# A hybrid attention layer on one core: first piece of x in two halves, a shorter warm-up, own raw buffers for the MLP weights, and other numbers in the order planner

## The chip, the cores and the metric

The kernel runs on one core of one Trainium2 chip. The metric is the time of one execution on the device in microseconds (us), of which three were taken. The profile is of one more execution, whose own time stands beside its span (the time from the first to the last instruction of the program).

## The reference: what is computed

One layer of a decoder over 512 tokens of width 1024, in float32. The input x is scaled by an RMS norm and projected once; the 3420 columns of the projection are split between two groups of eight heads of 64 that work side by side.

Group A is a native sparse attention. Each query attends three times: to 31 compressed keys, to selected blocks of 64 keys, and to a sliding window. With 512 tokens there are 8 blocks and up to 16 may be selected, and the window is 512 long, so that both of the last two are plain causal attention with keys and values of their own. The compressed keys and values come from two small networks (MLPs): 32 tokens of 64 numbers are put in a row, multiplied by a 2048 x 256 matrix, passed through SiLU and multiplied by a 256 x 64 matrix. Sigmoid gates weigh the three results.

Group B attends to the 128 keys per query that an indexer picks: four small heads of q x k, a relu, a weighted sum of the heads, then the 128 largest.

```
proj = rms_norm(x, norm_gain) @ w_in
o_nsa = g0 * o_cmp + g1 * o_sel + g2 * o_win;   o_nsa = o_nsa * silu(z_n)
score = sum_h relu(qi_h @ ki.T * 64**-0.5) * wi_h * 4**-0.5;   keys = top_k(score, 128)
o_dsa = attention(qd, kd[keys], vd[keys]) * silu(z_d)
out = x + concat(o_nsa, o_dsa) @ w_out
```

Queries and keys have an RMS norm and rotary positions.

## The kernel before, in words

Every product is made of three: each operand is split into a high part, rounded to the fp32r type by a copy, and a low part, the difference. High times high, high times low and low times high are added in PSUM. So each weight that arrives in a raw buffer costs one ScalarE copy (the high part, L356) and one subtraction on GpSimd or VectorE (the low part, L357) before TensorE can use it.

The program starts with the projection I (the indexer's keys and queries, L479). x arrives already transposed, in eight blocks k of 128 rows, each in one row with the 348 columns of the weights I for that block. The first block comes as one transfer with the norm's gains (`xw0`, L454), the others in five transfers (L352). For each block ScalarE makes the high part of x times gain (L466), ScalarE the square of x (L469), VectorE the running sum of the squares (L471), VectorE the low part (L473), and both the two parts of the weights (L475, L476); then come twelve products, for four tiles of 128 tokens. Ten products on a tile of zeros (`WARM`, L443) run on TensorE before the first block is there. The sum of the squares gives the norm's scale, which is applied to results later on.

After that the program projects chunks of columns in turn: C (input of the MLPs), B (keys and values of group A), Q1 and Q2 (queries), D, and Z0 to Z3 (the gates of the output). Between them stand the MLPs (`hidden`, L776, with the weights that `load_w1` brings in eight pieces of 256 KB for each of the two networks), the indexer (L689 to L704), attention, and at the end the output projection (L1219) with its own weights. Raw weights share one ring of four buffers (`raw`, `RAWB`); the MLPs' split weights have four tiles of four blocks each for both networks together, so that the second network's can be written only as the first's have been used.

Attention goes through units (a kind, a tile of 128 queries, a group of heads). For each unit the scores (L1010) are masked, exponentiated (L987) and scaled (L1000), the probabilities are transposed on TensorE (L1029), copied to a high part `pth` by ScalarE (L1030, or L1025 for the compressed keys) and a low part `ptl` (L1031), and multiplied with the values (L1040). `pth` and `ptl` have `TBUFS` buffers each. Mixed tiles (`mx`, L1198 to L1200) go into the output projection.

The order of the instructions is not that of the text. `set_order` (L112 onwards) collects all instructions with their dependences, those through the rings of buffers too, and plays the program forwards and backwards several times with a cost for each instruction, a latency between each pair of engines and a model of the transfers; each engine takes the ready instruction that is due first. The numbers above the function weigh this: `SPARE` is extra time between a producer and a product on TensorE, `PORT` a charge for VectorE and GpSimd when they want the port that they share, `SOON` how far ahead an engine looks for something more pressing, `PAUSE` a gap in the interleaving of the indexer. The best order found is made fixed: within each engine the instructions run in exactly that order, and a late operand holds up all that stands behind it. SyncE (SP) issues all the transfers, in one queue and in such an order too.

Of the kernel before, what the change touches and what calls it, by code (L numbers as in the profile page):

```python
# [9 lines left out]
F32 = mybir.dt.float32  # L10
# [3 lines left out]
AF = mybir.ActivationFunctionType  # L14
# [48 lines left out]
ARENA = 3689  # L63
ARENA_R = 5376 - 1024

WARM = 10
RTB = 4

COST = 1 / 2400
TBUFS, AHEAD, LAG = 3, 2, 2  # L70
R0, X0, L0 = 1.0, 0.5, 2.0
RA, X1, X2, X3, X4 = 0.2, 0.32, 0.4, 0.5, 0.2
PAUSE, LEAD, RAWB, W1B = 2.0, 8.0, 4, 8

MAGIC = float(0x5F3759DF)

# [7 lines left out]
    ("SP", "PE"): 900, ("SP", "DVE"): 950, ("SP", "Activation"): 900, ("SP", "Pool"): 950,  # L84
}

URGENT, SOON = 3000, 300
PE_URGENT, PE_SOON = 200, 60
ROUNDS = 8

# [2 lines left out]
LO_DVE = {"C": range(2)}  # L93

WBUFS = 4
PORT = 10

TURN = {"Activation": 125, "DVE": 118}

CHOICE = 0.0  # L100

SPARE = 200

HURRY = {}

# [3 lines left out]
def set_order(tc):  # L109
# [120 lines left out]
    def turns(due, back=False):  # L230


        to, frm = (before, after) if back else (after, before)
        left = [len(b) for b in frm]
        ready = [0.0] * count
        idle = defaultdict(float)
        waiting = defaultdict(list)
        for k in range(count):
            if not left[k]:
                waiting[eng[k]].append(k)  # L240
        order = defaultdict(list)
        start = [0.0] * count
        last = {e: () for e in TURN}
        if not back:
            due = [d - h for d, h in zip(due, hurry)]
            for k in reversed(range(count)):
                for j in before[k]:
                    due[j] = min(due[j], due[k] - costs[j][0])
        there = [0.0] * LANES
        for _ in range(count):  # L250
            now, e = min((max(idle[e], min(ready[k] for k in l)), e) for e, l in waiting.items() if l)
            l = waiting[e]

            late = max(idle["port"] - now, 0)
            k = min((k for k in l if ready[k] <= now), key=lambda k: due[k] + PORT * late * port[k]
                    + (CHOICE * TURN[e] if e in TURN and rows[k] != last[e] else 0))
            soon, urgent = (PE_SOON, PE_URGENT) if e == "PE" else (min(SOON, costs[k][0]), URGENT)

            u = min((q for q in l if now < ready[q] < now + soon), key=lambda q: due[q], default=None)
            if u is not None and due[u] + urgent < due[k]:  # L260
                k = min((q for q in l if ready[q] <= now and now + costs[q][0] <= ready[u] + 50),
                        key=lambda q: due[q], default=u)
            l.remove(k)
            start[k] = max(idle[e], ready[k], idle["port"] if port[k] else 0)
            if by[k] == "SP" and not back:
                start[k] = max(start[k], there[0])
            more = 0
            if e in TURN:
                if rows[k] != last[e]:
                    more = max(TURN[e] - (start[k] - idle[e]), 0)  # L270
                last[e] = rows[k]
            end = idle[e] = start[k] + costs[k][0] + more
            if port[k]:
                idle["port"] = end
            if by[k] == "SP":
                if back:
                    idle["transfers"] = max(idle["transfers"], start[k]) + costs[k][1]
                    end = max(end, idle["transfers"]) + 650
                else:
                    end = max(end + 650, idle["transfers"]) + costs[k][1]  # L280
                    idle["transfers"] = end
                    there = there[1:] + [end + 900]
            if back:
                start[k] = -end
            order[e].append(k)
            for q in to[k]:
                left[q] -= 1
                j, i = (q, k) if back else (k, q)
                ready[q] = max(ready[q], idle[e] if j in behind[i] else end + gap(j, i))
                if not left[q]:  # L290
                    waiting[eng[q]].append(q)
        return max(idle.values()), order, start
# [16 lines left out]
def tile_hybrid_layer(ctx, tc, xT, x, ng, win, gains, peT, w1, b1, w2, wout, cst, out):  # L309
# [39 lines left out]
    def load_raw(src, shape, name, where=None):  # L349
        tag, bufs = where or ("raw", RAWB)  # L350
        v = wp.tile(shape, F32, tag=tag, name=name, bufs=bufs)
        nc.sync.dma_start(v, src)  # L352
        return v
# [97 lines left out]

    n = S + nI
    xw0 = wp.tile([128, KB + n], F32, tag="xw0", name="xw0", bufs=1)
    nc.sync.dma_start(xw0, ng)  # L454
    ngt = xw0[:, :KB]
    pieces = [(0, 1, xw0[:, None, KB:])]

# [4 lines left out]
    acc = None  # L462
    for k0, k1, xw in pieces:
        for k in range(k0, k1):
            r, raw = xw[:, k - k0, :S], xw[:, k - k0, S:]
            nc.scalar.activation(hT["hi"][:, k, :], r, AF.Copy, scale=ngt[:, k:k + 1])  # L466

            sq = work.tile([128, S], F32, tag="xsq", name=f"xsq{k}", bufs=3)
            nc.scalar.activation(sq, r, AF.Square)  # L469
            if k:  # L470
                nc.vector.tensor_tensor(sq, sq, acc, op=ALU.add)  # L471
            acc = sq
            nc.vector.scalar_tensor_tensor(hT["lo"][:, k, :], r, ngt[:, k:k + 1],  # L473
                                           hT["hi"][:, k, :].bitcast(F32), op0=ALU.mult, op1=ALU.subtract)
            (nc.scalar.copy if k else nc.vector.tensor_copy)(hi[:, k, :], raw)  # L475
            nc.vector.tensor_tensor(lo[:, k, :], raw, hi[:, k, :].bitcast(F32), op=ALU.subtract)  # L476
            for a, b in ((hT["hi"], hi), (hT["lo"], hi), (hT["hi"], lo)):
                for t in range(NT):
                    nc.tensor.matmul(Ips[t][:, :NI[t]], a[:, k, t * 128:(t + 1) * 128], b[:, k, :NI[t]],  # L479
                                     start=(k == 0 and b is hi and a is hT["hi"]), stop=(k == KB - 1 and b is lo))  # L480
# [35 lines left out]

    def tables(j, name):
        gn = gns[:, j, None, :]
        c, s = (work.tile([128, NT, HD], F32, tag="tab" + x, name="tab" + x, bufs=3) for x in "cs")
        nc.gpsimd.tensor_tensor(c, cosd, gn[:, :, :HD].to_broadcast([128, NT, HD]), op=ALU.mult)  # L520
        nc.gpsimd.tensor_tensor(s, sind, gn[:, :, HD:].to_broadcast([128, NT, HD]), op=ALU.mult)
        return c, s
# [209 lines left out]

    def load_w1(kv):
        for j in range(8):
            raw = load_raw(w1[:, kv, 2 * j:2 * j + 2, :], [128, 2, 256], f"raw_w1{kv}{j}")
            if j % 2 == 0:
                pair = [w1_tile(kv, j, x) for x in range(2)]
            w1t[kv, j] = [v[:, 2 * (j % 2):2 * (j % 2) + 2] for v in pair]
            split(raw, *w1t[kv, j], nc.gpsimd)
# [568 lines left out]
def _layouts(inp):  # L1308
# [17 lines left out]
    w1 = [tile_k(np.asarray(inp[n])[0]) for n in ("cmp_k_w1", "cmp_v_w1")]  # L1326
    b1 = [np.asarray(inp[n])[0] for n in ("cmp_k_b1", "cmp_v_b1")]
    w2 = [tile_k(np.asarray(inp[n])[0]) for n in ("cmp_k_w2", "cmp_v_w2")]
    xw = np.concatenate([tile_k(np.ascontiguousarray(x.T)), chunks[0].reshape(128, KB, -1)], axis=2)
    return {  # L1330
        "xT": np.ascontiguousarray(xw[:, 1:]),
        "x": np.ascontiguousarray(x),
# [66 lines left out]
```

## Time and profile before

| | us |
|---|---|
| median of three runs | 316.26 (315.95 to 316.64) |
| the profiled execution's own time | 316.42 |
| its span | 314.6 |
| TensorE (PE) busy | 306.6 |
| VectorE (DVE) busy | 261.1 |
| ScalarE (ACT) busy | 242.3 |
| GpSimd (POOL) busy | 234.1 |

A busy share is the time in which an engine had an instruction in work, over the span. Matmuls overlap one another, so a product of 0.39 us can be followed by the next one 0.23 us later. The granted clock of TensorE reads 1.00 in all the 40 slices of the page.

### The profile page before, as it was taken

What the parts mean: (1) busy time and instruction counts of PE and PEld (TensorE: products, weight loads), DVE (VectorE), ACT (ScalarE), POOL (GpSimd) and SP (SyncE); (2) the same over time, 40 slices, a digit from 0 to 9 for tenths busy, and PEclk for the clock granted to TensorE, in tenths of its full rate; (3) what the DMA queues carried; (4) which work ended last, traced back from release to release, by engine and by line L of the source; (5) the groups of instructions that cost most, each with busy time, mean ns of one, the idle gap of its engine ahead of it and who ended that gap; (6) DMA issues with size and microseconds to landing.
All of it is one profiled execution on the core that took longest, in us unless ns stands there. A gap on an engine that the chain in (4) does not pass through costs nothing.

```text
span 314.6 us, 6043 instructions
## 1 busy us (share of the span) xinstructions
PE 306.6 (97%) x1681; PEld 258.9 (82%) x1681; DVE 261.1 (83%) x797; ACT 242.3 (77%) x794; POOL 234.1 (74%) x416
## 2 busy tenths in 40 slices
PE   8999999899999999999999999999999999999995
PEld 5998888789877888888887888888888888888885
DVE  4996624689999999999999999999999999886501
ACT  5971666778999899899999989883379998996500
POOL 2079989799885499995899889766877995667500
PEclk9999999999999999999999999999999999999999
DMA  7990365656510033320040044042435242003011
GB/s 259 417 322 4 98 172 144 173 163 170 165 40 1 0 83 92 97 85 3 3 133 3 4 134 134 2 124 72 135 106 163 70 151 76 20 0 133 2 67 67
DMA packets 21249, 32.16 MB, mean 102 GB/s; under 512 B 5664, under 2 KB 8480, under 8 KB 21216
## 3 DMA queue, kind: packets, MB, share of 16 engines
q1 hardware_dynamic: 21216, 31.78, 33.2%
q8 instruction: 13, 0.21, 0.3%
q14 instruction: 20, 0.16, 0.2%
HBM read 29.04 MB, written 2.47 MB: 100 GB/s over the span
## 4 chain that ended last, share of the span: by engine, by line
PE 81%; ACT 7%; DMA 4%; POOL 3%; issue 2%; DVE 1%; SPq 1%; POOLq 0%; DVEq 0%
PE out L1219 14%; PE z L400 14%; PE D L390 7%; PE on L1040 7%; PE s_n L1010 6%; PE T_n L1029 6%; PE Q L390 5%; PE I L479 5%; DMA raw_w<-in_w_dram 4%; PE C L400 3%; PE od L1040 3%; PE T_d L1029 3%; PE s_d L1010 3%; POOL w1l L357 2%; PE I L443 1%
## 5 line engine op out<-in xcount | busy, mean ns | idle before, releaser
L987 ACT ACTIVATE P_n<-P_n,arena 128x416 f32<-128x416 f32 (+9 forms) x64 | 33.5, 525 | 3.3 <-DVE arena L982 2.8
L1000 POOL TENSOR_SCALAR P_n<-P_n,arena 128x416 f32<-128x416 f32 (+7 forms) x64 | 30.4, 493 | 1.1
L982 DVE CUSTOM_DVE_ANT_0 P_n<-s_n,arena 128x416 f32<-128x416 f32 (+9 forms) x64 | 30.3, 489 | 0.5
L1031 DVE TENSOR_TENSOR ptl<-T_n,pth 128x512 fp32r<-128x512 f32 x40 | 27.4, 684 | 1.8 <-ACT pth L1030 1.3
L1010 PE MATMUL s_n<-kn,arena_r 128*128 128x288 f32 (+12 forms) x116 | 28.3, 328 | 0.5 <-DVE arena_r L621 0.5
L700 DVE MAX8 m<-scores 128x8 f32<-128x512 f32 (+2 forms) x48 | 26.6, 554 | 0.5
L1029 PE MATMUL T_n<-arena,P_n 128*128 128x128 f32 x160 | 26.9, 272 | 0.0
L701 DVE MATCH_REPLACE8 scores<-m,scores 128x512 f32<-128x512 f32 (+2 forms) x48 | 26.1, 544 | 0.1
L400 PE MATMUL z<-hThi,whi_Z 128*128 128x512 f32 x64 | 25.7, 404 | 0.0
L400 PE MATMUL z<-hThi,wlo_Z 128*128 128x512 f32 x64 | 25.3, 398 | 0.0
L400 PE MATMUL z<-hTlo,whi_Z 128*128 128x512 f32 x64 | 25.2, 397 | 0.0
L1030 ACT CAST pth<-T_n 128x512 fp32r<-128x512 f32 x40 | 23.4, 587 | 1.9 <-PE T_n L1029 1.4
L1010 PEld LDWEIGHTS s_n<-kn,arena_r 128*128 128x128 f32 x116 | 20.7, 188 | 4.6 <-DVE arena_r L621 0.7
L1029 PEld LDWEIGHTS T_n<-arena,P_n 128*128 128x128 f32 x160 | 20.3, 140 | 4.8 <-POOL P_n L1000 0.2
L1219 PE MATMUL out<-wohi,mx 128*128 128x512 f32 (+1 forms) x72 | 23.9, 378 | 0.0
L1219 PE MATMUL out<-whi_wo,mx 128*128 128x512 f32 (+1 forms) x72 | 23.6, 379 | 0.0
L357 POOL TENSOR_TENSOR wlo_Z<-raw_Z,whi_Z 128x512 fp32r<-128x512 f32 x16 | 20.4, 1295 | 3.6 <-ACT whi_Z L356 3.5
L390 PE MATMUL Q<-whi_Q,hThi 128*128 128x256 f32 (+1 forms) x64 | 22.4, 349 | 0.0
L357 POOL TENSOR_TENSOR w1l<-raw_w,w1h 128x512 fp32r<-128x512 f32 x16 | 20.5, 1289 | 2.4 <-DMA raw_w<-in_w_dram 1.3
L390 PE MATMUL Q<-whi_Q,hTlo 128*128 128x256 f32 (+1 forms) x64 | 22.2, 347 | 0.0
L390 PE MATMUL Q<-wlo_Q,hThi 128*128 128x256 f32 (+1 forms) x64 | 21.8, 340 | 0.0
L1040 PE MATMUL on<-ptl,arena_r 128*128 128x512 f32 x48 | 20.0, 417 | 0.0
(264 smaller groups left out, 1099.2 us busy)
## 6 DMA issues: line engine op xcount, KB each, us to landing
raw_w<-in_w_dram SPq DMA_DIRECT2D x16, 256.0 KB, 3.1
raw_Z<-in_win_dram SPq DMA_DIRECT2D x16, 256.0 KB, 3.0
wor<-in_wout_dram SPq DMA_DIRECT2D x16, 256.0 KB, 2.8
raw_Q<-in_win_dram SPq DMA_DIRECT2D x12, 256.0 KB, 2.8
raw_D<-in_win_dram SPq DMA_DIRECT2D x8, 256.0 KB, 3.0
xres<-in_x_dram SPq DMA_DIRECT2D x8, 256.0 KB, 2.8
out_dram<-xres SPq DMA_DIRECT2D x7, 256.0 KB, 2.0
xw<-in_xT_dram SPq DMA_DIRECT2D x2, 860.0 KB, 8.8
```

Of the source, the lines that this page charges most:

```text
L357: engine.tensor_tensor(lo, raw, hi.bitcast(F32), op=ALU.subtract)
L390: nc.tensor.matmul(out_ps, a[:, k, tsl], b, start=(k == 0 and b is hi and a is hT["hi"]), stop=(k == KB - 1 and a is hT["lo"]))
L400: nc.tensor.matmul(out_ps, b[:, csl], a[:, k, :], start=(k == 0 and b is hi and a is hT["hi"]), stop=(k == KB - 1 and b is lo))
L700: nc.vector.max(m8, sc)
L982: nc.vector.tensor_tensor_reduce(P, src_, mask, u.r[:, b:b + 1], 3e38, op0=ALU.add, op1=ALU.min, accum_out=m[:, b:b + 1])
L987: nc.scalar.activation(P, P, AF.Exp, bias=m[:, b:b + 1], scale=-1.0, accum_out=l[:, b:b + 1])
L1000: nc.gpsimd.tensor_scalar(Pb, Pb, l[:, bb:bb + 1], 1.0 if u.gate is not None else 0.5, op0=ALU.mult, op1=ALU.mult)
L1010: nc.tensor.matmul(p, q[0][:, b], k[:, x], start=(x == 0), stop=(x == 1))
L1029: nc.tensor.transpose(p[:, h * 128:(h + 1) * 128], u.P[:, h, j * 128:(j + 1) * 128], ident)
L1031: nc.vector.tensor_tensor(pl, p, ph.bitcast(F32), op=ALU.subtract)
L1040: nc.tensor.matmul(o, u.v[j], pp, start=(u.first and j == 0 and x == 0), stop=(end and x == 1))
L1219: nc.tensor.matmul(p, a, b[:, csl], start=(k == 0 and b is hi and a is mx[0]), stop=(k == 7 and a is mx[1]))
```

## The change

The transfer of the first block of x is cut in two, the weights I now stand ahead of x in each block, and the first half holds gains, weights and 256 of the 512 columns of x. For the first block the high and the low part of x are made in two halves as well. The squares of x get six buffers instead of three. The warm-up has nine products. The pieces of the MLPs' weights get a ring of four raw buffers of their own. `TBUFS` goes from three to two, and the two tables of rotary factors become one tile. In the planner a transfer that is not queued behind another lands later by 0.7 of its time, and `PAUSE`, `SOON`, `PORT` and `SPARE` have other values.

```diff
--- before.py
+++ after.py
@@ -63,14 +63,14 @@
 ARENA = 3689
 ARENA_R = 5376 - 1024
 
-WARM = 10
+WARM = 9
 RTB = 4
 
 COST = 1 / 2400
-TBUFS, AHEAD, LAG = 3, 2, 2
+TBUFS, AHEAD, LAG = 2, 2, 2
 R0, X0, L0 = 1.0, 0.5, 2.0
 RA, X1, X2, X3, X4 = 0.2, 0.32, 0.4, 0.5, 0.2
-PAUSE, LEAD, RAWB, W1B = 2.0, 8.0, 4, 8
+PAUSE, LEAD, RAWB, W1B = 3.0, 8.0, 4, 8
 
 MAGIC = float(0x5F3759DF)
 
@@ -84,7 +84,7 @@
     ("SP", "PE"): 900, ("SP", "DVE"): 950, ("SP", "Activation"): 900, ("SP", "Pool"): 950,
 }
 
-URGENT, SOON = 3000, 300
+URGENT, SOON = 3000, 200
 PE_URGENT, PE_SOON = 200, 60
 ROUNDS = 8
 
@@ -93,13 +93,13 @@
 LO_DVE = {"C": range(2)}
 
 WBUFS = 4
-PORT = 10
+PORT = 14
 
 TURN = {"Activation": 125, "DVE": 118}
 
 CHOICE = 0.0
 
-SPARE = 200
+SPARE = 250
 
 HURRY = {}
 
@@ -277,7 +277,7 @@
                     idle["transfers"] = max(idle["transfers"], start[k]) + costs[k][1]
                     end = max(end, idle["transfers"]) + 650
                 else:
-                    end = max(end + 650, idle["transfers"]) + costs[k][1]
+                    end = max(end + 650 + 0.7 * costs[k][1], idle["transfers"]) + costs[k][1]
                     idle["transfers"] = end
                     there = there[1:] + [end + 900]
             if back:
@@ -451,7 +451,8 @@
 
     n = S + nI
     xw0 = wp.tile([128, KB + n], F32, tag="xw0", name="xw0", bufs=1)
-    nc.sync.dma_start(xw0, ng)
+    for c in (slice(0, KB + nI + S // 2), slice(KB + nI + S // 2, KB + n)):
+        nc.sync.dma_start(xw0[:, c], ng[:, c])
     ngt = xw0[:, :KB]
     pieces = [(0, 1, xw0[:, None, KB:])]
 
@@ -462,16 +463,19 @@
     acc = None
     for k0, k1, xw in pieces:
         for k in range(k0, k1):
-            r, raw = xw[:, k - k0, :S], xw[:, k - k0, S:]
-            nc.scalar.activation(hT["hi"][:, k, :], r, AF.Copy, scale=ngt[:, k:k + 1])
-
-            sq = work.tile([128, S], F32, tag="xsq", name=f"xsq{k}", bufs=3)
+            raw, r = xw[:, k - k0, :nI], xw[:, k - k0, nI:]
+            halves = [slice(0, S)] if k else [slice(0, S // 2), slice(S // 2, S)]
+            for c in halves:
+                nc.scalar.activation(hT["hi"][:, k, c], r[:, c], AF.Copy, scale=ngt[:, k:k + 1])
+
+            sq = work.tile([128, S], F32, tag="xsq", name=f"xsq{k}", bufs=6)
             nc.scalar.activation(sq, r, AF.Square)
             if k:
                 nc.vector.tensor_tensor(sq, sq, acc, op=ALU.add)
             acc = sq
-            nc.vector.scalar_tensor_tensor(hT["lo"][:, k, :], r, ngt[:, k:k + 1],
-                                           hT["hi"][:, k, :].bitcast(F32), op0=ALU.mult, op1=ALU.subtract)
+            for c in halves:
+                nc.vector.scalar_tensor_tensor(hT["lo"][:, k, c], r[:, c], ngt[:, k:k + 1],
+                                               hT["hi"][:, k, c].bitcast(F32), op0=ALU.mult, op1=ALU.subtract)
             (nc.scalar.copy if k else nc.vector.tensor_copy)(hi[:, k, :], raw)
             nc.vector.tensor_tensor(lo[:, k, :], raw, hi[:, k, :].bitcast(F32), op=ALU.subtract)
             for a, b in ((hT["hi"], hi), (hT["lo"], hi), (hT["hi"], lo)):
@@ -516,7 +520,8 @@
 
     def tables(j, name):
         gn = gns[:, j, None, :]
-        c, s = (work.tile([128, NT, HD], F32, tag="tab" + x, name="tab" + x, bufs=3) for x in "cs")
+        tab = work.tile([128, 2, NT, HD], F32, tag="tab", name="tab", bufs=3)
+        c, s = tab[:, 0], tab[:, 1]
         nc.gpsimd.tensor_tensor(c, cosd, gn[:, :, :HD].to_broadcast([128, NT, HD]), op=ALU.mult)
         nc.gpsimd.tensor_tensor(s, sind, gn[:, :, HD:].to_broadcast([128, NT, HD]), op=ALU.mult)
         return c, s
@@ -732,7 +737,7 @@
 
     def load_w1(kv):
         for j in range(8):
-            raw = load_raw(w1[:, kv, 2 * j:2 * j + 2, :], [128, 2, 256], f"raw_w1{kv}{j}")
+            raw = load_raw(w1[:, kv, 2 * j:2 * j + 2, :], [128, 2, 256], f"raw_w1{kv}{j}", where=("raww", 4))
             if j % 2 == 0:
                 pair = [w1_tile(kv, j, x) for x in range(2)]
             w1t[kv, j] = [v[:, 2 * (j % 2):2 * (j % 2) + 2] for v in pair]
@@ -1326,7 +1331,7 @@
     w1 = [tile_k(np.asarray(inp[n])[0]) for n in ("cmp_k_w1", "cmp_v_w1")]
     b1 = [np.asarray(inp[n])[0] for n in ("cmp_k_b1", "cmp_v_b1")]
     w2 = [tile_k(np.asarray(inp[n])[0]) for n in ("cmp_k_w2", "cmp_v_w2")]
-    xw = np.concatenate([tile_k(np.ascontiguousarray(x.T)), chunks[0].reshape(128, KB, -1)], axis=2)
+    xw = np.concatenate([chunks[0].reshape(128, KB, -1), tile_k(np.ascontiguousarray(x.T))], axis=2)
     return {
         "xT": np.ascontiguousarray(xw[:, 1:]),
         "x": np.ascontiguousarray(x),
```

## Rows read from the trace of the kernel before

**Rows 1.** The page's busy times (share of the span) xinstructions.

```profile
PE 306.6 (97%) x1681; PEld 258.9 (82%) x1681; DVE 261.1 (83%) x797; ACT 242.3 (77%) x794; POOL 234.1 (74%) x416
```

**Rows 2.** Windows: length; busy (instructions) of PE, PEld, DVE, ACT, POOL; clock, DMA, GB/s.

```profile
60.00:290.00 230.00, 226.58 (x1259) 191.37 (x1258) 216.48 (x679) 198.87 (x681) 185.78 (x349) 1.00 0.29 82
20.00:60.00 40.00, 40.00 (x197) 33.26 (x197) 22.16 (x75) 21.82 (x72) 37.75 (x44) 1.00 0.46 133
```

**Rows 3.** Timeline of TensorE: start, duration, instruction, and [idle before, who ended it].

```profile
60.78 0.28 PE L390 MATMUL Q<-whi_Q,hTlo 128*128 128x256 f32 x1
62.35 0.73 PE L689 MATMUL idx<-kix,arena_r 128*128 128x512 f32 x2 [1.29 <-DVE scores L695]
...
70.04 0.28 PE L776 MATMUL hid<-w1h,FS 128*128 128x256 f32 x1
71.09 0.61 PE L689 MATMUL idx<-kix,arena_r 128*128 128x384 f32 x2 [0.78 <-DVE scores L695]
```

**Rows 4.** The chain that ended last: start, duration, what.

```profile
295.22 16.15 PE out L1219 x93
```

**Rows 5.** Timeline, GpSimd and TensorE at the end.

```profile
299.16 0.74 POOL L1200 TENSOR_TENSOR mx<-od_d,mx 128x256 fp32r<-128x256 f32 x1 [0.52 <-ACT mx L1199]
...
305.61 0.40 PE L1219 MATMUL out<-wohi,mx 128*128 128x512 f32 x1
```

**Rows 6.** Timeline of ScalarE, 57 to 69.

```profile
57.44 0.62 ACT L356 CAST w1h<-raw_w 128x512 fp32r<-128x512 f32 x1 [1.01 <-DMA raw_w<-in_w_dram]
...
59.33 0.62 ACT L356 CAST w1h<-raw_w 128x512 fp32r<-128x512 f32 x1 [0.58 <-DMA raw_w<-in_w_dram]
...
60.07 1.07 ACT L691 ACTIVATE idx<-idx 128x512 f32<-128x512 f32 x2
...
68.46 0.62 ACT L356 CAST w1h<-raw_w 128x512 fp32r<-128x512 f32 x1 [1.24 <-DMA raw_w<-in_w_dram]
```

**Rows 7.** Timeline of SyncE's transfers, 51 to 55.

```profile
51.22 0.33 SPq L657 DMA_DIRECT2D dr_gate<-arena  x1
53.08 1.28 SPq L660 DMA_DIRECT2D arena<-dr_gate  x3
54.41 0.43 SPq L352 DMA_DIRECT2D raw_w<-in_w_dram  x1
```

**Rows 8.** The tile raw_w: its 16 transfers, issue to landing.

```profile
DMA to landing us min/median/max: 2.6/3.1/4.7
```

**Rows 9.** Timeline of TensorE at the start.

```profile
1.38 4.30 PE L443 MATMUL I<-arena 128*128 128x512 bf16 x10 [1.38 <-DVE arena L445]
...
5.26 1.01 PE L479 MATMUL I<-whi_I,hThi 128*128 128x92 f32 x4
...
6.11 0.75 PE L479 MATMUL I<-whi_I,hTlo 128*128 128x92 f32 x4
...
9.06 0.76 PE L479 MATMUL I<-whi_I,hThi 128*128 128x92 f32 x4
```

**Rows 10.** Timeline of ScalarE at the start.

```profile
4.05 0.72 ACT L466 ACTIVATE hThi<-xw 128x512 fp32r<-128x512 f32 x1 [1.84 <-DMA xw<-in_ng_dram]
...
7.46 0.72 ACT L466 ACTIVATE hThi<-xw,xw 128x512 fp32r<-128x512 f32 x1 [0.65 <-DMA xw<-in_xT_dram]
8.09 0.47 ACT L475 CAST whi_I<-xw 128x348 fp32r<-128x348 f32 x1
```

**Rows 11.** Transfers: count, KB each, median us from issue to landing.

```profile
xw<-in_ng_dram SPq DMA_DIRECT2D x1, 434.0 KB, 3.3
```

**Rows 12.** Timeline, first and last of 42 copies with the product two parts before.

```profile
113.08 0.48 PE L1040 MATMUL on<-ptl,arena_r 128*128 128x512 f32 x1
113.18 0.62 ACT L1030 CAST pth<-T_n 128x512 fp32r<-128x512 f32 x1
...
286.70 0.62 ACT L1025 CAST pth<-pd 128x512 fp32r<-128x512 f32 x1 [0.58 <-DVE pd L1023]
...
288.41 0.39 PE L1040 MATMUL on<-ptl,arena_r 128*128 128x512 f32 x1
```

## The prediction

> **What bounds the kernel now.** I read the busy shares first, then the idle places of the busiest engine one by one, then what ended each, and last the end of the program. TensorE is busy 306.6 of 314.6 us [rows 1], so at most 8.0 us of idle can be taken away without removing products. The reader should split these 8.0: 1.38 before the first product [rows 9]; 3.2 behind the last one, which ends at 295.22 + 16.15 = 311.37 [rows 4]; 1.29 and 0.78 in front of two indexer products [rows 3]; and 8.0 - 1.38 - 3.2 - 2.07 = 1.35 in smaller places. So this is a TensorE program with two holes of note. The next engine is VectorE: 216.48 of 230 us between 60 and 290, but 22.16 of 40 before that, while GpSimd has 37.75 of those 40 [rows 2]. It is not the bound yet: the last mixed tile of attention is ready at 299.16 + 0.74 = 299.90 and TensorE takes it at 305.61 [rows 5], so attention may end up to 5.7 us later before the end moves.
>
> The two holes have one cause. TensorE stands before the products of 62.35 and 71.09 because VectorE's score sums came late [rows 3]; these wait for ScalarE's relu. ScalarE works its queue in order, and in front of the two relus of 60.07 stand two casts of MLP weights (57.44 and 59.33) that waited 1.01 and 0.58 us for their transfers; the cast of 68.46 waited 1.24 [rows 6]. Together 1.59 us late before a hole of 1.29, and 1.24 before one of 0.78: each delay is longer than its hole. The transfers were late because they were issued late: the second network's pieces share a ring of four raw buffers with the Q pieces ahead of them, and SyncE stood behind the gate's store (51.22) and its first reloads (53.08, 1.28 us long) before it issued the first piece at 54.41 [rows 7]. A piece takes 2.6 to 4.7 us to land [rows 8].
>
> **The change part by part.** *Own raw buffers for the MLP weights, later landings in the planner, more spare time before a product.* With a ring of their own the first four pieces of the second network wait for the first network's casts alone, no longer for the Q pieces, and the planner, which now adds 0.7 of a transfer's time to its landing, has a reason to place them ahead of the gate's store on SyncE. Both act on the 1.01, 0.58 and 1.24. If the waits go, the sums are in time and the two holes close: -1.29 - 0.78 = -2.07 us, with 0 and -2.07 as bounds. I take all of it, since each delay exceeds its hole by 0.30 and 0.46. What is late next in that stretch: GpSimd's low parts of the same weights, as GpSimd has little idle before 60 [rows 2]; they feed the hidden products, which the planner can set behind Q products whose weights are there.
>
> *First piece in two halves, warm-up of nine.* Ten warm-up products start at 1.38 and take 4.30, and the first real one starts at 5.26 [rows 9]: 0.43 each. One fewer lets the real ones start at 4.83. Are their operands there? The whole piece (434 KB) landed in 3.3 us [rows 11], ScalarE and VectorE start on it at 4.05 [rows 10]. A piece of 256 KB lands in 2.6 at best [rows 8], so by a straight line through the two the first 306 KB need 2.8, half a microsecond less: work starts at about 3.55, and the half cast is shorter than the whole one's 0.72 [rows 10]. So yes. But the gain of 0.43 is not kept whole, for two reasons. First, the opening group of four products took 6.11 - 5.26 = 0.85, while the five groups to 9.06 took 0.59 each [rows 9]: TensorE is still at its lower level (512 columns in 0.43 us is 1.2 GHz) when it begins them, and an earlier start puts more of them there, at half the speed. Second, the third piece lands only at 7.46, where ScalarE stood idle 0.65 us for it, its weight cast ends at 8.09 + 0.47 = 8.56 and its products start at 9.06 [rows 10, 9]: with the hand-off between engines inside that 0.50, only part of it can be gained. Bounds 0 and -0.43; I take -0.2.
>
> The Trainium skill, "DMA: Bandwidth & Descriptors", section "Rules for kernel authors", speaks against a split: large transfers for bandwidth, small ones gathered into one. By its section on the anatomy of one DMA (2.0 us fixed plus bytes at 436 GB/s) my estimate is 2.7 us for the first half. Here the rule costs nothing by the rows: the wait at 7.46 is for bytes of later pieces, both halves are far over the size that the rule calls small, and the sum would stay -0.2 by either.
>
> The split adds one ScalarE copy, one VectorE subtraction and one SyncE issue. ScalarE's lie in front of its idle 0.65 [rows 10]. VectorE's second start is at most another whole instruction of 0.75; that one is in the way of the products only if the lagging sums do not make room, and with six square buffers they may. The five transfers of x behind it are issued one slot later, while bytes are already queued. I take 0 for all three; without cover it would be the rest of the 0.43.
>
> *Two transposed buffers in place of three.* A copy of transposed probabilities must now wait for the product that reads the part two before it. The trace shows both orders free of that: the first copy that breaks the new rule starts at 113.18 while that product runs until 113.08 + 0.48 = 113.56, the last starts at 286.70 while its product ends at 288.41 + 0.39 = 288.80; counting through, 42 of the 66 copies with such a product do [rows 12]. The wait would stand in ScalarE's queue in front of the exponentials of the next unit, and VectorE and GpSimd wait for those. The planner sees the rule and can pull the products forward, because TensorE has z and output products to put elsewhere; attention has 5.7 us to spare at the end. Bounds: 0, and at the other end four new holes of the mean of the two known ones, (1.29 + 0.78) / 2 = 1.03, so +4.1. I take +0.3, near the lower end, for the spare time.
>
> *The rest* (merged table tile, swapped columns, the port's and the look-ahead's weights, the longer pause) adds no instruction and only reorders: 0, within the bounds just named.
>
> **Sum.** The profiled execution took 316.42, 1.8 us more than its span and 0.16 more than the median. 316.42 - 2.07 - 0.2 + 0.3 = 314.45, and against the median of 316.26 that is **314.3 us**.
>
> **The rivals.** *Reordered, nothing gained.* The raw ring was not what set the issue times: the second network's cast tiles come free only when the first network's products have run, so the casts stay late or other late transfers take their place in ScalarE's queue. For it: GpSimd's full load before 60 [rows 2], which no buffer changes. Against it: the three waits name the transfer and no other engine [rows 6]. Then -0.2 alone remains: 316.1.
>
> *Slower, by the two buffers.* Every attention part now couples TensorE, ScalarE and VectorE within two parts, and an order fixed in advance turns each misjudged duration into a hole. For it: 42 of 66 places; VectorE at 94% from 60 to 290 [rows 2]. Against it: TensorE's filler and the 5.7 us. It decides from three holes on, as 2.27 / 1.03 = 2.2; with four the time is 316.26 - 2.27 + 4.1 = 318.1.
>
> *More gained.* The new order also closes the smaller 1.35 us and pays nothing for the buffers: 316.26 - 2.27 - 1.35 = 312.6.
>
> **How the numbers follow.** Forecast 0.50 (its own range 313.3 to 315.3), more gained 0.14, nothing gained 0.19, slower 0.17. Within 0.2% is 315.6 to 316.9, about what a measurement can tell from no change. Nothing gained lies inside it, but some of its outcomes are below 315.6: faster 0.50 + 0.14 + 0.06 = 0.70, same 0.13, slower 0.17. The range for 8 in 10 runs from 312.5, just under the case of more gained, to 317.1, which leaves out most of the slower case and little else.
>
> **What would show it.** Right: no ScalarE cast of the second network waits over 0.3 us for its transfer, the first of its pieces is issued before the gate's store, TensorE's idle places between 60 and 72 sum to under 0.5, the first real product starts at about 4.85 and the last at most 2.5 us earlier than now. Wrong: the same casts still wait for transfers; ScalarE's copies of transposed parts stand behind products and new holes over 0.5 us lie between 100 and 290; or the last mixed tile is taken by TensorE as soon as it is there, which would mean that attention has become the bound.

## The result

The changed kernel takes 313.40 us (median of five runs, 313.09 to 314.2), the kernel before 315.95 in the same comparison (315.0 to 316.64): a ratio of 0.9926, with a 95% interval of 0.99 to 0.9951. Its profiled execution took 313.09 us, with a span of 311.3; that of before had 316.42 and 314.6. In the changed kernel's rows every line of the code below stands one to five numbers further down: L479 is L483, L689 is L694, L691 is L696, L1219 is L1224; `load_raw`, L352, and the casts, L356, kept theirs.

The page's busy times after, for [rows 1]:

```profile
PE 306.0 (98%) x1680; PEld 258.7 (83%) x1680; DVE 261.8 (84%) x798; ACT 241.2 (77%) x795; POOL 234.5 (75%) x416
```

The chain that ended last, for [rows 4]:

```profile
291.90 16.02 PE out L1224 x93
```

TensorE is idle for 311.3 - 306.0 = 5.3 us instead of 8.0: 1.38 before its first instruction, as before, 311.3 - 307.92 = 3.38 behind its last (3.2 before), and 0.54 in all other places, where it was 2.07 in the two holes and 1.35 elsewhere. The remaining 0.6 of the 3.3 us of span is busy time, one warm-up product (0.43) among it.

Where the idle time went is read from windows of TensorE alone (length; busy (instructions); clock; DMA share; GB/s). Before:

```profile
60.00:75.00 15.00, 12.93 (x96) 1.00 0.54 149
75.00:100.00 25.00, 24.43 (x142) 1.00 0.33 92
100.00:200.00 100.00, 99.22 (x535) 1.00 0.22 61
```

After:

```profile
60.00:75.00 15.00, 15.00 (x125) 1.00 0.43 133
75.00:100.00 25.00, 24.67 (x133) 1.00 0.23 65
100.00:200.00 100.00, 100.00 (x539) 1.00 0.22 61
```

The stretch with the two holes is full, and so is the long one behind it. The waits of TensorE name the places (total us, times, longest). Before:

```profile
PE idx L689 <- DVE scores L695: 2.1, 2, 1.3
...
PE qT_ps L611 <- issue: 0.8, 1, 0.8
PE s_n L1010 <- DVE arena_r L621: 0.5, 1, 0.5
```

After:

```profile
PE I L443 <- DVE arena L445: 1.4, 1, 1.4
PE I L483 <- ACT whi_I L479: 0.2, 1, 0.2
PE T_n L1034 <- POOL P_n L1005: 0.2, 1, 0.2
```

The line of idx is what the prediction counted; the lines of qT_ps and s_n, 0.8 and 0.5, are nearly all of what it called smaller places, and they went too. Both short waits of 0.2 are new: one at the start, in the second block of x, and one before a transposition (T_n).

ScalarE's casts of both networks' weights waited for transfers eight times before, 5.6 us in all (total us, times, longest):

```profile
ACT w1h L356 <- DMA raw_w<-in_w_dram: 5.6, 8, 1.2
```

After, ScalarE's waits have no such line. The first and the last cast of the second network's weights, for [rows 6]; none of the eight has a bracket, so none waited:

```profile
57.77 0.62 ACT L356 CAST w1h<-raw_w 128x512 fp32r<-128x512 f32 x1
...
70.11 0.62 ACT L356 CAST w1h<-raw_w 128x512 fp32r<-128x512 f32 x1
```

SyncE after, for [rows 7]: twelve of the sixteen pieces, four of the second network's eight among them, are issued ahead of the gate's store, and the last four behind its reloads.

```profile
52.39 0.33 SPq L662 DMA_DIRECT2D dr_gate<-arena  x1
...
54.28 1.37 SPq L665 DMA_DIRECT2D arena<-dr_gate  x3
...
58.54 4.04 SPq L352 DMA_DIRECT2D raw_w<-in_w_dram  x4
```

The start, for [rows 9 to 11]. TensorE:

```profile
1.38 3.83 PE L443 MATMUL I<-arena 128*128 128x512 bf16 x9 [1.38 <-DVE arena L445]
4.83 0.95 PE L483 MATMUL I<-whi_I,hThi 128*128 128x92 f32 x4
5.63 0.75 PE L483 MATMUL I<-whi_I,hTlo 128*128 128x92 f32 x4
...
7.21 0.85 PE L483 MATMUL I<-whi_I,hThi 128*128 128x92 f32 x4 [0.25 <-ACT whi_I L479]
...
9.09 0.76 PE L483 MATMUL I<-whi_I,hThi 128*128 128x92 f32 x4
```

ScalarE and SyncE's queue:

```profile
3.63 0.91 ACT L469 ACTIVATE hThi<-xw 128x256 fp32r<-128x256 f32 x2 [1.41 <-DMA xw<-in_ng_dram]
...
6.07 0.72 ACT L469 ACTIVATE hThi<-xw,xw 128x512 fp32r<-128x512 f32 x1 [1.01 <-DMA xw<-in_xT_dram]
```

```profile
1.64 2.32 SPq L352 DMA_DIRECT2D xw<-in_xT_dram  x5
```

For comparison the same two places in the kernel before:

```profile
5.20 0.71 ACT L466 ACTIVATE hThi<-xw,xw 128x512 fp32r<-128x512 f32 x1
```

```profile
1.17 2.34 SPq L352 DMA_DIRECT2D xw<-in_xT_dram  x5
```

The first half's transfer (count, KB, us from issue to landing):

```profile
xw<-in_ng_dram SPq DMA_DIRECT2D x1, 306.0 KB, 2.9
```

Work starts at 3.63 instead of 4.05 and the first product at 4.83 instead of 5.26, as it should. But the transfers behind the first piece are issued from 1.64 on, one slot later than before, and ScalarE has to wait for the second block of x until 6.07; before, it took that block at 5.20 without a wait. The third block's products start at 9.09; they started at 9.06.

### The profile page after: what moved, and what is told of

It is laid out like the page before. It is cut to its first block, busy times and chain, and to the rows that moved or that the text cites. A ratio compares the mean times of both kernels' runs of the same rounds, so it can differ in the third digit from the quotient of the medians.

```text
span 311.3 us, 6052 instructions
## 1 busy us (share of the span) xinstructions
PE 306.0 (98%) x1680; PEld 258.7 (83%) x1680; DVE 261.8 (84%) x798; ACT 241.2 (77%) x795; POOL 234.5 (75%) x416
## 4 chain that ended last, share of the span: by engine, by line
PE 81%; DVE 4%; POOL 4%; DMA 3%; ACT 3%; issue 3%; SPq 1%; DVEq 0%; POOLq 0%; ACTq 0%
PE out L1224 15%; PE z L400 14%; PE on L1045 7%; PE D L390 7%; PE T_n L1034 6%; PE B L390 5%; PE s_n L1015 5%; PE I L483 4%; PE C L400 4%; PE od L1045 3%; PE s_d L1015 3%; PE T_d L1034 3%; PE Q L390 2%; DMA xw<-in_xT_dram 1%; POOL w1l L357 1%
## 5 line engine op out<-in xcount | busy, mean ns | idle before, releaser
L400 PE MATMUL z<-hThi,whi_Z 128*128 128x512 f32 x64 | 26.4, 412 | 0.0
L1034 PE MATMUL T_n<-arena,P_n 128*128 128x128 f32 x160 | 26.1, 272 | 0.2 <-POOL P_n L1005 0.2
L1224 PE MATMUL out<-whi_wo,mx 128*128 128x512 f32 (+1 forms) x72 | 24.1, 382 | 0.0
L1224 PE MATMUL out<-wohi,mx 128*128 128x512 f32 (+1 forms) x72 | 23.9, 375 | 0.0
L1045 PE MATMUL on<-pth,arena_r 128*128 128x512 f32 x48 | 20.2, 421 | 0.0
```

The lines of the kernel that those rows point to most:

```text
L400: nc.tensor.matmul(out_ps, b[:, csl], a[:, k, :], start=(k == 0 and b is hi and a is hT["hi"]), stop=(k == KB - 1 and b is lo))
L1034: nc.tensor.transpose(p[:, h * 128:(h + 1) * 128], u.P[:, h, j * 128:(j + 1) * 128], ident)
L1045: nc.tensor.matmul(o, u.v[j], pp, start=(u.first and j == 0 and x == 0), stop=(end and x == 1))
L1224: nc.tensor.matmul(p, a, b[:, csl], start=(k == 0 and b is hi and a is mx[0]), stop=(k == 7 and a is mx[1]))
```

## The experiments

The planner answers every edit with another order, so an edit alone tells little of its own cost. Where it says "its own order", the order that the planner had found for that kernel was written into it as lists of instructions, and the planner was left out; only the named edit differs then. "Replanned" means that the planner was run on the edited kernel. All were timed in five rounds beside the kernel before, whose median was 315.88 us (316.11 in the last comparison).

**Are late issues the cause of the two holes?** The kernel before, its own order, and on SyncE alone two pieces of the second network moved ahead of the gate's reloads:

```diff
 SyncE, order around the gate
-store gate, reload, reload, reload, piece 0, reload, piece 1, pieces 2 to 7
+store gate, piece 0, reload, reload, reload, piece 1, reload, pieces 2 to 7
```

> The kernel before with its own order on all engines, written out as a list, but on SyncE the first piece of the second MLP's weights moved ahead of the gate's reloads and the second ahead of the last reload. No buffer, no product and no other order is changed. Theory (late weight transfers held up ScalarE, and so made both holes): the first cast loses its wait of 1.01 and the second its 0.58, the hole of 1.29 us before the product of 62.35 closes, the later hole of 0.78 shrinks too because the pieces behind follow earlier: 0.8 to 2.1 us faster than before, ratio 0.994 to 0.9975. Rival (the holes come from VectorE's load or the fixed order itself): within 0.3 us of before, ratio 0.999 to 1.001.

314.35 us (313.99 to 315.44), ratio 0.9962 [0.9945, 0.998]. SyncE, then the waits of TensorE:

```profile
50.10 0.42 SPq L657 DMA_DIRECT2D dr_gate<-arena  x1
50.58 0.42 SPq L352 DMA_DIRECT2D raw_w<-in_w_dram  x1
52.80 1.28 SPq L660 DMA_DIRECT2D arena<-dr_gate  x3
54.17 0.38 SPq L352 DMA_DIRECT2D raw_w<-in_w_dram  x1
```

```profile
PE qT_ps L611 <- issue: 0.8, 1, 0.8
PE s_n L1010 <- DVE arena_r L621: 0.6, 1, 0.6
```

The line of idx is gone, the other two stand as before. Not one buffer was added and no other engine's order was touched, so the issue times on SyncE are shown to be the cause of the two holes. One of the eight casts still waited for its transfer (0.67 us, at 66.05), with no hole behind it. Closing the holes is worth 1.5 us by the medians and 1.2 by the ratio, inside the expected range.

**The new start alone.** The kernel before, its own order:

```diff
-WARM = 10
+WARM = 9
-    nc.sync.dma_start(xw0, ng)
+    for c in (slice(0, KB + nI + S // 2), slice(KB + nI + S // 2, KB + n)):
+        nc.sync.dma_start(xw0[:, c], ng[:, c])
```

with the copies of the first block in two halves and the columns swapped; the squares keep three buffers.

> The kernel before with its own order on all engines, and of the change only the start: first piece in two halves behind its weights, halves of the high and low part, nine warm-up products (the squares keep three buffers). Theory as forecast: 0.2 us faster. Rival, from the trace of the changed kernel, in which the second piece of x landed at 6.07 and the third block's products began at 9.09 where they began at 9.06 before: the later issue of the transfers behind eats all of it, 0.0 us, or up to 0.2 slower.

317.02 us (316.21 to 317.78), ratio 1.0041 [1.0022, 1.0059]: alone, the new start makes the kernel slower, and by more than the rival allowed. Its trace is of the fastest of the seven executions (316.21) and does not show the loss. Two runs take the start apart. The first has nine warm-up products and the old transfer, the second ten and the two halves.

> The kernel before, its own order, with nine warm-up products in place of ten and nothing else. Theory (start_only's 1.1 us come from the transfers): within 0.2% of the kernel before, 315.3 to 316.5 us. Rival (they come from the shorter warm-up: TensorE idles before its first product and its granted clock rises later, which makes the first products longer): 316.7 to 317.2 us.

316.07 us (315.18 to 316.54), ratio 1.0002 [0.9987, 1.0016].

> The kernel before, its own order, with the first piece of x in two halves behind its weights and ten warm-up products. Theory (start_only's loss comes from the transfers): 316.6 to 317.2 us, with the second piece used about 0.7 us later than before. Rival (it comes from the shorter warm-up): 315.6 to 316.2 us.

316.61 us (315.92 to 318.31), ratio 1.0021 [1.0006, 1.0037]. So most of the loss comes with the transfers, and the shorter warm-up neither costs nor gains. Why it gains nothing is to be seen in TensorE's timeline with nine products:

```profile
8.74 0.76 PE L479 MATMUL I<-whi_I,hThi 128*128 128x92 f32 x4
...
62.30 0.73 PE L689 MATMUL idx<-kix,arena_r 128*128 128x512 f32 x2 [1.55 <-DVE scores L695]
```

The third block starts 0.32 earlier than before, and the indexer product behind the first hole starts at 62.30, where it started at 62.35 [rows 3]: the hole has grown from 1.29 to 1.55 and swallowed the gain, since its end is set by SyncE's transfers, and the second network's first piece is issued at 54.35 here and at 54.41 before. With the halves it goes the other way (ScalarE, then TensorE):

```profile
6.59 0.72 ACT L469 ACTIVATE hThi<-xw,xw 128x512 fp32r<-128x512 f32 x1 [1.54 <-DMA xw<-in_xT_dram]
```

```profile
7.74 0.86 PE L483 MATMUL I<-whi_I,hThi 128*128 128x92 f32 x4 [0.50 <-ACT whi_I L479]
...
9.62 0.60 PE L483 MATMUL I<-whi_I,hThi 128*128 128x92 f32 x3
...
63.07 0.73 PE L693 MATMUL idx<-kix,arena_r 128*128 128x512 f32 x2 [1.30 <-DVE scores L699]
```

The second block is used 1.39 later than before (6.59 against 5.20; expected was about 0.7), the third block's products start 0.56 later, and this loss is still there at the indexer (63.07), as the transfers have moved with it: the second network's first piece is issued at 55.59.

**The start inside the changed kernel.** The changed kernel's own order with one transfer and ten warm-up products:

> The changed kernel with its own order of instructions, but with the first piece of x again in one transfer and ten warm-up products. Theory (the extra transfer of the new start sets back the second piece of x, 5.2 to 6.1 us, and start_only measured 1.1 us slower than the kernel before): faster than the changed kernel by 0.3 to 1.1 us, 312.3 to 313.1 us, and the products of the second block follow the first without a hole. Rival (the start is worth nothing either way, since the third block's products began at 9.06 and 9.09 us): 313.2 to 313.6 us. Second rival (the start does gain inside the changed kernel, start_only lost by something else): 313.8 us or more.

313.51 us (312.98 to 313.77), ratio 0.9916 [0.9896, 0.9937], against 0.9926 [0.99, 0.9951] with the new start. The rival is right: inside the changed kernel the new start is worth nothing either way. The third block starts at 9.13 here, and TensorE does not wait before the second.

The changed kernel's own order with the second half issued from ScalarE's queue, so that SyncE issues the rest as early as before:

```diff
-    for c in (slice(0, KB + nI + S // 2), slice(KB + nI + S // 2, KB + n)):
-        nc.sync.dma_start(xw0[:, c], ng[:, c])
+    c0, c1 = slice(0, KB + nI + S // 2), slice(KB + nI + S // 2, KB + n)
+    nc.sync.dma_start(xw0[:, c0], ng[:, c0])
+    nc.scalar.dma_start(xw0[:, c1], ng[:, c1])
```

> The changed kernel with its own order, but the second half of the first piece is issued from ScalarE's queue, so that SyncE issues the five transfers of x behind it one slot (0.47 us) earlier, as in the kernel before. Theory (the later issue is what delays the second piece of x from 5.2 or earlier to 6.07, and makes the hole of 0.25 to 0.4 us in front of its products): the second piece lands 0.3 to 0.5 us earlier, the hole goes, the kernel is 0.2 to 0.5 us faster than the changed one. Rival (bytes, not issue, set the landing): it lands at about 6.0 again and the time is the changed kernel's within 0.2 us.

313.38 us (313.0 to 313.81), ratio 0.9919 [0.9901, 0.9937]. ScalarE, then TensorE:

```profile
4.05 0.91 ACT L470 ACTIVATE hThi<-xw 128x256 fp32r<-128x256 f32 x2 [1.40 <-DMA xw<-in_ng_dram]
...
5.38 0.71 ACT L470 ACTIVATE hThi<-xw,xw 128x512 fp32r<-128x512 f32 x1
```

```profile
4.83 1.37 PE L484 MATMUL I<-whi_I,hThi 128*128 128x92 f32 x4
6.04 0.75 PE L484 MATMUL I<-whi_I,hTlo 128*128 128x92 f32 x4
```

The second block is used at 5.38 without a wait, so the later issue was what delayed it, and TensorE's wait of 0.25 before its products is gone. The first half is now used at 4.05, exactly as the whole piece was, but the first product still starts at 4.83. That the third block starts at 9.00, hardly earlier than 9.09, has another reason: the opening group of products took 6.04 - 4.83 = 1.21 in this execution and 5.63 - 4.83 = 0.80 in that of the changed kernel. The Trainium skill, "DMA: Bandwidth & Descriptors", section "Rules for kernel authors", says that spreading transfers over several issuing engines saves the sequencer's time of issue and no bandwidth. The trace agrees: 0.69 us sooner for the second block and 0.42 later for the first.

**Two buffers of transposed products.** The changed kernel's own order with `TBUFS` back at three:

> The changed kernel with its own order written out, but three buffers for the transposed probabilities instead of two: no other order, only the waits of the copies for the product two parts before are gone. As forecast, these waits cost some 0.3 us: ratio to before 0.990 to 0.992. Rival (the planner had already put the products early enough): no difference from the changed kernel beyond 0.2 us, ratio 0.992 to 0.9935.

313.82 us (313.51 to 314.37), ratio 0.9934 [0.9916, 0.9952]. In that order the two buffers cost nothing. What they do is to be seen on ScalarE in the changed kernel (busy, mean ns, idle before and what ended most of it):

```profile
L1035 ACT CAST pth<-T_n 128x512 fp32r<-128x512 f32 x40 | 23.1, 581 | 1.0 <-PE od L1045 0.8
```

One copy waited 0.8 us for a product, a wait that the run with three buffers does not have, and TensorE lost nothing by it.

**The own ring and the planner's numbers.** First the changed kernel without the own ring, replanned:

```diff
-            raw = load_raw(w1[:, kv, 2 * j:2 * j + 2, :], [128, 2, 256], f"raw_w1{kv}{j}", where=("raww", 4))
+            raw = load_raw(w1[:, kv, 2 * j:2 * j + 2, :], [128, 2, 256], f"raw_w1{kv}{j}")
```

> The changed kernel without the MLP weights' own raw buffers (they share the ring of four again), planned anew with the change's numbers. The planner's numbers alone gave a ratio of 0.9951 and the own ring alone 0.9895. Theory (ring and numbers close the same two holes): the time of the numbers alone, plus what the new start costs: 314.2 to 315.4, ratio 0.9945 to 0.999. Rival (the ring adds nothing once the planner lands transfers later): the changed kernel's time, ratio 0.991 to 0.994.

317.54 us (316.89 to 318.44), ratio 1.0053 [1.0032, 1.0074]: slower than the kernel before, and 4.1 us slower than with the ring. Neither expectation held. The holes of 60 to 75 are closed here too; a longer one opened later. TensorE, and windows from there on:

```profile
95.87 1.64 PE L1015 MATMUL s_n<-kn,arena_r 128*128 128x448 f32 x4 [1.90 <-DVE arena_r L626]
```

```profile
92.00:96.00 4.00, 2.10 (x17) 1.00 0.19 36
96.00:98.00 2.00, 2.00 (x6) 0.54 0.04 1
98.00:99.00 1.00, 1.00 (x3) 0.50 0.00 0
99.00:100.00 1.00, 1.00 (x5) 0.72 0.00 0
```

The hole of 1.90 us costs more than itself: behind it the granted clock is at its lower level (0.50, which is 1.2 GHz) until past 99, and the missing shares of the clock, 2 x 0.46 + 0.50 + 0.28, make 1.70 us of lost work on top. Not every execution had this: the mean granted clock was 0.993 to 0.995 in four of the seven, which took 317.54 to 318.44 us, and 0.999 in the other three, which took 316.89 to 317.14. So the fall of the clock goes with about 1 us of the 4.1, and most of the loss is there without it.

Then the kernel before with the new planner numbers alone, replanned:

```diff
-PAUSE, LEAD, RAWB, W1B = 2.0, 8.0, 4, 8
+PAUSE, LEAD, RAWB, W1B = 3.0, 8.0, 4, 8
-URGENT, SOON = 3000, 300
+URGENT, SOON = 3000, 200
-PORT = 10
+PORT = 14
-SPARE = 200
+SPARE = 250
-                    end = max(end + 650, idle["transfers"]) + costs[k][1]
+                    end = max(end + 650 + 0.7 * costs[k][1], idle["transfers"]) + costs[k][1]
```

> The kernel before with only the planner's numbers of the change (later landings, longer pause, smaller look-ahead, larger port charge, more spare time), planned anew: shared raw ring, three transposed buffers, old start. If the order alone closes the holes: 1.5 to 2.5 us faster, ratio about 0.993 to 0.995. If the own ring is needed: within 0.8 us of before. A new order may also cost up to 1 us elsewhere.

314.24 us (313.7 to 315.0), ratio 0.9951 [0.9934, 0.9968]. TensorE waits for no score sums; one wait is left behind the start, 0.8 us before a product of s_n. SyncE issues the second network's pieces from 49.08 on here, and the gate's store only at 93.33: the store is out of their way.

The kernel before with the own ring and the merged table tile (without which the buffers don't fit), the old numbers, the old start and three transposed buffers, replanned:

```diff
-        c, s = (work.tile([128, NT, HD], F32, tag="tab" + x, name="tab" + x, bufs=3) for x in "cs")
+        tab = work.tile([128, 2, NT, HD], F32, tag="tab", name="tab", bufs=3)
+        c, s = tab[:, 0], tab[:, 1]
-            raw = load_raw(w1[:, kv, 2 * j:2 * j + 2, :], [128, 2, 256], f"raw_w1{kv}{j}")
+            raw = load_raw(w1[:, kv, 2 * j:2 * j + 2, :], [128, 2, 256], f"raw_w1{kv}{j}", where=("raww", 4))
```

> The kernel before with own raw buffers for the MLP weights and the merged table tile (without which it does not fit in SBUF), old numbers in the planner, planned anew, three transposed buffers, old start. If the own ring closes the holes by itself: 1.5 to 2.3 us faster, ratio 0.993 to 0.995. If it needs the planner's later landings to be used: within 0.8 us of before.

**312.48 us** (312.29 to 312.63), ratio 0.9895 [0.9878, 0.9912]: the best of all, with all its runs below all of the changed kernel's. All of TensorE's waits:

```profile
PE I L443 <- DVE arena L445: 1.4, 1, 1.4
```

The gain of 3.4 us is above the expected 1.5 to 2.3. Each of the two alone closes the two holes, and in the order planned for it the own ring alone closes every place. Two runs ask why the changed kernel, which has both, is 0.9 us behind. The changed kernel with the old start, replanned:

> The changed kernel with the old start (one transfer for the first piece, ten warm-up products), ordered anew by the planner with the changed numbers, two buffers of transposed products and the own ring. Theory (the start costs the changed kernel something, and ring_replanned at 312.48 us was better only for its old start): 312.3 to 313.0 us. Rival (the order that the old numbers give is the better one beside the own ring, whatever the start): 313.2 to 314.0 us, with waits of TensorE that ring_replanned does not have.

313.13 us (312.82 to 313.36), ratio 0.9906 [0.9883, 0.9928], between the two expected ranges. And the changed kernel with the old numbers, replanned:

> The changed kernel (new start, own ring, two buffers of transposed products) ordered by the planner with the numbers of before. ring_replanned (own ring, old start, three buffers, the same old numbers) gave 312.48 us, old_start_replanned (own ring, old start, two buffers, new numbers) 313.13 us. Theory (beside the own ring the old numbers give the better order): 312.3 to 312.8 us. Rival (the third buffer of transposed products made ring_replanned better): 313.2 to 314.0 us, with TensorE waiting for transposed products somewhere.

313.55 us (313.49 to 314.2), ratio 0.9927 [0.9912, 0.9942]. In this last run the theory fell: beside the ring, the new start and two buffers the old numbers are not the better ones. Nor is the rival shown, since TensorE waits nowhere for the transposed buffers; behind its first product it waits 0.2 and 0.2. The seven kernels timed with the own ring lie between 312.48 and 313.82 us. From which part the last microsecond comes isn't settled: replanned orders differ throughout, and the listed waits are too small to account for it.

## Why the prediction was right, and where not

The forecast of 314.3 us was 0.9 above the measured 313.40, inside its range and on the right side. By its steps:

**The two holes** (-2.07, all of it taken): right in cause and in trace. The three waits of [rows 6] are gone, the second network's first four pieces are issued before the gate's store, and 60 to 75 is full. sp_order_only shows the cause by itself. In time the holes gave 1.2 to 1.5 us rather than 2.07 there; the profiled execution of before took 316.42, 0.5 above the median of 315.88 over 23 runs, so its holes may have been longer than usual. That the ring and the planner's side both act was right too: in the kernel before, either the ring or the five new numbers together are enough. The later landings were not run by themselves. The prediction gave the ring and the numbers one joint gain, and what the ring adds depends on the order: without it the changed kernel, planned anew, ends 4.1 us higher, although the two holes are closed there too.

**The start** (-0.2): this step failed. The first product does begin at 4.83 as forecast. The step that was wrong is "The five transfers of x behind it are issued one slot later, while bytes are already queued. I take 0 for all three". The slot is 1.64 - 1.17 = 0.47 us, and the second block of x came at least 0.87 later (6.07 against 5.20 in the trace before, where ScalarE did not wait for it), so that TensorE waited in front of it, and the third block's products started at 9.09. The slot is not the whole of this delay; the rest stays open. Of the six traces with both halves on SyncE four have this wait of TensorE, 0.22 to 0.50 us long; of those with one transfer none has it. In the changed kernel the term is 0 (313.40 against 313.51); in the kernel before it is +1.1 us for the whole start and +0.7 for the halves alone, outside the bounds of 0 and -0.43. The landing of the first half was forecast well: 2.8 us by the straight line, 2.9 in the trace. The estimate of 2.7 from the Trainium skill came as near, though the page, "DMA: Bandwidth & Descriptors", section "Anatomy of one DMA — SWDGE (gpsimd) path", gives its figure for transfers that GpSimd issues, and SyncE issued these. The rule of the Trainium skill that the prediction weighed ("DMA: Bandwidth & Descriptors", section "Rules for kernel authors": gather small transfers into one) pointed to the right side, though the pieces are larger than those it calls small, and part of what it cost here was the queue's slot: with the second half on the other queue the second block was used at 5.38.

**Two transposed buffers** (+0.3): 0 in the order that was planned for them, as the run with three shows. The count of 42 was too high. It pairs the copies with the products that read `ptl` ([rows 12] show two of these), but a copy writes `pth`, and of the two products it waits only for the one that reads `pth`; paired in order of time with those it is 33 of 66, the first at 120.52, while that product starts at 120.90. In the changed kernel the same count is 5, so the planner did pull the products forward, which the prediction had as its reason for staying near the lower end. Whether it gave up something elsewhere for that isn't shown.

**The smaller places** (nothing taken): mis-sized. The prediction put 1.35 us there and left them as they were, except in the rival "more gained". They were two waits, 0.8 for the rotated queries of group B and 0.5 for a part of Q. In the changed kernel 0.54 - 0.25 = 0.29 is left behind the start. That is -1.06. They stood in sp_order_only and are gone in ring_replanned, so the new order closes them; which part of the change it needs for that isn't shown.

With these sizes the sum is 316.42 - 2.07 + 0 + 0 - 1.06 = 313.29 against the profiled 313.09. The rest of 0.2 is no idle time: the same products behind the start of the third block took 0.35 us less busy time in the execution after (311.37 - 9.06 - 3.42 = 298.89 before, 307.92 - 9.09 - 0.29 = 298.54 after), and 0.15 more passed behind the last one. That the forecast came within 0.9 us is in part luck: -0.2 and +0.3, both 0 in fact, nearly cancel, and if the holes gave only 1.2 to 1.5 us, that error lies the other way from the smaller places left out.

Of the rivals, "nothing gained" fell with the holes, and "slower, by the two buffers" with the full stretch from 100 to 200. "More gained" (312.6) had the mechanism of the smaller places right; the measured time lies between it and the forecast. Of the prediction's signs of being right one failed: the last product ends 311.37 - 307.92 = 3.45 us earlier and not at most 2.5, by the smaller places. The bound that it named as its third sign of error did not come: GpSimd, after, has the last mixed tile ready at 295.79 + 0.74 = 296.53, and output products run on TensorE without a break from 291.90 on, so TensorE is still the bound. GpSimd's last such instruction, for [rows 5]:

```profile
295.79 0.74 POOL L1205 TENSOR_TENSOR mx<-od_d,mx 128x256 fp32r<-128x256 f32 x1 [0.52 <-ACT mx L1204]
```

## What to carry to other kernels

Where one queue issues all transfers in a fixed order, a hole on the busiest engine can be mended by moving two issues; look there before adding buffers. Microseconds saved at the start are worth nothing as long as a later hole ends at a time that transfers set: close the holes first, and only then measure the start. Split a first transfer only if nothing behind it in the same queue is needed soon, for every issue moves all the later ones; and in a planned order time each part alone with the order held fixed, since replanning alone can move the total as much as the part does.

## What was not expected of the hardware

The same ten warm-up products took between 3.73 us (planner_only) and 4.45 us (ring_replanned) from one execution to another, and the products behind them went on slower or faster, while the granted clock reads 1.00 throughout in these rows: the opening group took 5.73 - 4.89 = 0.84 us in the first and 6.70 - 5.26 = 1.44 in the second, where later ones took 0.59. TensorE's timeline of planner_only, then of ring_replanned:

```profile
1.38 3.73 PE L443 MATMUL I<-arena 128*128 128x512 bf16 x10 [1.38 <-DVE arena L445]
```

```profile
1.38 4.45 PE L443 MATMUL I<-arena 128*128 128x512 bf16 x10 [1.38 <-DVE arena L445]
5.26 1.65 PE L479 MATMUL I<-whi_I,hThi 128*128 128x92 f32 x4
6.70 1.08 PE L479 MATMUL I<-whi_I,hTlo 128*128 128x92 f32 x4
...
9.99 0.20 PE L479 MATMUL I<-whi_I,hThi 128*128 128x92 f32 x1
```

In the latter's trace the third block of x starts only at 9.99, and it is still the fastest kernel. This scatter at the start is larger than what the new start could gain. The Trainium skill, "TensorE: Matmul & The Clock Gate", section "What's actually happening", says that the moment at which the clock rises varies by half a microsecond either way; the rows agree.

Behind a hole of 1.90 us the granted clock fell to 0.54 and 0.50 for some three microseconds (after_shared_ring), so that in this execution it cost nearly twice its length. TensorE had no other idle time between 92 and 96: 4.00 - 2.10 = 1.90. The holes of 1.29 and 0.78 in the kernel before and that of 1.55 in warm_nine_only had no such cost: the clock reads 1.00 from 60 to 75 in both.
